# A ring of its own for the attention's squares, a product with ones for the second tokens' roots, and a new stored order in a two-layer hybrid encoder

## The chip, the cores and the metric

The kernel runs on one core of one Trainium2 chip. The metric is the device time of one execution in microseconds (us); several executions are timed and their median is given. The core has five engines that work side by side, each with its own instruction queue that is served in order: TensorE (PE: matmuls, and PEld for the load of their stationary operand), VectorE (DVE), ScalarE (ACT), GpSimd (POOL) and SyncE (SP), which in this kernel issues every DMA. Matmuls write to PSUM banks of 512 f32 per partition; everything else lives in SBUF or in device memory.

## The reference, cut to what matters

Two layers over 2,048 tokens of width 1,024. Each layer normalises x by the root of its mean square, scales and shifts it, projects it, and runs two groups of heads beside each other: four heads of gated linear attention (GLA), and four heads of differential softmax attention. Both outputs are normalised, gated, joined and projected back.

```python
h = rms_norm(x, norm_g[l]) * (1.0 + scale[:, None]) + shift[:, None]
proj = h @ w_in[l]
gq, gk, gv, glr, gz, dq, dk, dv, dz = split_columns(proj)
...
o_diff = diff_branch(dq, dk, dv, dz, qn_g[l], kn_g[l], lam, lam_init, diff_norm_g[l])
y = jnp.concatenate([o_gla, o_diff], axis=-1).astype(x.dtype) @ w_out[l]
x = x + gate[:, None] * y
```

In the differential group a head's output is the difference of two softmax maps times v, and two lines of it matter here: the output is divided by the root of its mean square, and the gate dz goes through a SiLU.

```python
attn = p[:, :, 0] - lam * p[:, :, 1]
...
o = rms_norm(o, g_out) * (1.0 - lam_init)
return o.reshape(B, S, DIFF_WIDTH) * jax.nn.silu(z.astype(f32))
```

## The kernel before, in words

**Tiles and stages.** The tokens are cut into four units u of 512, and each layer l runs over the units in turn; key = l * 4 + u counts them. For one unit the normalised input h is kept transposed, as eight tiles of 128 features by 512 tokens, each as a rounded part hhi and a remainder hlo; every weight tile w is split in the same way into hi and lo, so one product of the reference is three matmuls here. Seven projections ("items") follow: items 0 to 3 are the four softmax heads (q, k, v and gate of one head side by side, 512 columns), 4 and 5 the inputs of GLA's convolution, 6 GLA's gate. Items 7 and 8 are the output projection. The order of the items in a unit is 0, 4, 1, 2, 5, 3, 6.

**PSUM.** There are two rings of four banks: acc for the dense products, and one shared by sc (scores), tp (transposes) and po (attention outputs). Each item fills four acc banks, one per 128 tokens. The next dense product can only start in a bank that its reader has left.

**Emptying a head's banks** (head_evac). For each of the four banks t: ACT copies q and k to rw and v to Vt, ACT takes the tanh of the gate's 128 columns into a tile th, and DVE forms z = (th + 1) * gate, which reads th and the bank. That is the last use of the bank. The tile th is taken from a ring with the tag "th" of two buffers of 128 by 128.

**The end of an attention block** (pv, in attn_gen). For each 128 queries qt, once the output o_ stands in a po bank, ACT squares it with a running sum, and writes the squares, which nobody reads, to a tile junk:

```python
junk = p_t.tile([P, P], F32, tag="th", name="junk", bufs=2)
ss = p_sm.tile([P, 2], F32, tag="oss", name="oss")
A.activation(junk, o_, AF.Square, accum_out=ss[:, 0:1])
```

It is taken from the same ring as th. POOL then raises the sum to the power -1/2 (wq), and DVE scales o_ by it into z.

**Roots of the input** (root, rs_write, prep_gen, start). The sum of squares of a unit's tokens comes as 128 partitions by 4. root scales it on DVE (xms) and takes the power -1/2 on POOL into columns 0 to 3 of a constant tile rs128 (rs in the profile). The roots are wanted along the free axis and alike on all partitions, as a tile rsb of 128 by 512. Two ways lead there:
- rs_write: PE transposes rs128 into a tp bank, DVE copies four rows of it (xrr), SP writes these 2 KB to device memory (rd), and later, in prep_gen, SP reads them back broadcast over the partitions into rsb. Every unit but the first uses this way. For the units of layer 0 the squares are taken in prep_gen itself on ACT, from x; for layer 1 they come from the output projection of layer 0 (out_gen).
- in start, for the first unit: DVE multiplies an identity by the roots (dg, a tile of the ring t2 of three buffers), PE multiplies ones by dg in f32 into a tp bank, and ACT copies the bank to rsb.

Then make_h builds h: DVE multiplies x by the gain and rsb (xp), ACT rounds it with the shift added to hhi, DVE forms hlo.

**The order of the work.** The program isn't issued as it is written. Six streams (q and k preparation, attention, GLA, preparation of h, modulation, dense products) are run by a small scheduler that records each operation; Program.record keeps its reads and writes. Then Program.order plans: each engine takes the ready operation with the smallest turn, and a ring's buffers are handed out strictly in the order in which the program was recorded, so that of one tag no tile is started before those recorded ahead of it have their buffers. The turns come from the constant ORDER, a packed list of one step per recorded operation, if its length is that of the program. The result is the fixed instruction stream of each engine. In the profile nearly every instruction therefore has the same line, L362, where issue() calls the engines, and is told apart by its tiles.

```python
left_out = {t: list(q) for t, q in turn.items()}
slots = {t: [{} for _ in range(q[0].bufs or q[0].pool.bufs)] for t, q in turn.items()}
...
ahead = left_out[t].index(b, 0, 2) if b in left_out[t][:2] else N
if len(slots[t]) <= ahead or new.get(t, 0) and ahead != new[t]:
    blocked[t].append(i)
    break
```

Of the kernel before, what the change touches and what calls it, by code (L numbers as in the profile page):

```python
# [1338 lines left out]
def _layouts(x, c, w_ada, b_ada, norm_g, w_in, conv_w, w_gk, b_gk, gla_norm_g, qn_g, kn_g, lam_q1, lam_k1, lam_q2,  # L1339
# [30 lines left out]
    'gYDtAcd_peLW-sAb~<1OPH_YYOsRCU1+iqMG@NhME8jT~h%dSx#q=f&Vff-&-1vJ$o%JUz`%A6x<-6i;XUXaMEK+WB2HPPjBcg*He*HK>@DOV{bX'  # L1370
    'L)U`d>_!D7kqr{-sQQg5wx%r<@z%SHFs^SN3QCTp(od#lW$fWhs_9p*`e4DocfvT<lX_N1?6M>*0ozVNdlL;=I=Nwk?L{FL~MX*rABpWknIKSu=^'
    'ks__?b5$4HazYU$YWoV|hv(QklnpCp$RQS1*69OF~-c5|3tj+JE-|&J9Iu>yNxCa`7z`X8N;lYA(dVO*qoyuCTM>p4jf652C$`Wccn`A(3cGhD9#'
    'P-c^m|TGN%7=#PXrs=qUcm?qcIbHQ^B#mRW&%GNU^R6DuB2YL+#Me*osp`!S9@S#GS^mpAmZ=i;KqT|TgDsxj8=A1cz_<fCY%IjaXgvQg@_F|nGi'
    '0ED=oLn`kgIrqR;Om7!i>q0OI?XmOM;3_Ln@fqhb=Yn;`7E5Vm(9b5*3|_UZEZi^bpG5Z%ycbw~wxZ)i+zW9yR4AwvtRyuYzs3pC7`2}e`?+<LSh'
    'a%B<H@MrXRNau^EAJ^5u&HBBsOJMmj>ye;hLNdte7b~fQYv)8zNdKYoMXixB2OfyNiPt2jG?9=4Rqid{T55=C)D|{*Bm-yc0}VZ@rXaqe--HwL<@'
    '&P5){cRglrufBcZ<e|WlnF9y-BZrScrLDc_4PPBl3Q($xa;q5gT8j+kS@qj}qskxx23l1|B_ghw%ints^FmyQmwy02!|d*EO?hpipkY0ul|{>zv{'
    'xxXBk0;Ge+`SU?|)&b@3s7c?NM_H+9$lA!Ri82uW0y-gDUX0q2zhO}^UvN60|63Zr#BI0`rB`wa!Ck9MR5fbH4Yc&G~_<WDL*gl-@@no^i!B4;Tp'
    'yMYJRFHu&f%UIW44%r?^j?4jZa&~o-i`XlFq?7<5*NN&6Z`l-&?1G!6{~%P{lnXDNR0D^4mUdY;R1qPdF>vgjfgeh9!+~*By|QJcO3^52m<c|3DQ'
    'yY%l19b{dbw<>Vsi;$f?CWA!WO|oCplpEK~T={h6uM6cx$?tQ@c;6;2324XeeFHzamgZU4|zVMEj;#k-ayILW2Ml7_Blt+uEu42PP*28Q6I*Yx2$'
# [209 lines left out]
```

## Time and profile before

| what | value |
|---|---|
| median of 3 runs | 2417.67 us (2416.72 to 2417.84) |
| the profiled execution, whole | 2415.17 us |
| its span, first to last instruction | 2413.1 us |
| mean granted TensorE clock over the span | 0.996 |
| ACT busy | 1235.0 us (51%) |
| POOL busy | 121.1 us (5%) |
| DMA moved | 575.86 MB, mean 239 GB/s |

The profile is that of one execution. Each of its lines begins with a start time from the span's beginning and a length in us, then engine, line, operation, the tiles as out<-in by the program's names, the shape, and a count where like instructions were merged; in square brackets stands the idle time of the engine before it and what ended that. Matmuls overlap, so that the length of one is more than the distance from one to the next. Rows of the windows table begin with a stretch and its length, and tell for each engine how long it was busy in it and with how many instructions; after the engines come the granted TensorE clock as a share of full speed (PEclk), the busy share of the DMA engines, and GB/s. SPq is SyncE's queue of DMA issues.

### The profile page before, as it was taken

To read this page: it belongs to the slowest core of one execution; us is meant where nothing else is said; L and a number is where in the kernel's file an instruction comes from. 1 tells how busy PE (TensorE), PEld (TensorE's weight loads), DVE (VectorE), ACT (ScalarE), POOL (GpSimd) and SP (SyncE) were. 2 spreads that over 40 slices of the span, in tenths; PEclk is the share of its full clock that TensorE was granted. 3 is DMA by queue.
4 is the path that set the end of the run, shared out by engine and by line. 5 is a ranking of instruction groups with operands and counts; after the bars stand their busy time and mean duration, and the time that the engine had idled before them with its cause. 6 is when DMAs were issued, how large, how long until landed. Compare 5 with 4: busy or idle time off the path is not lost.

```text
span 2413.1 us, 38502 instructions
## 1 busy us (share of the span) xinstructions
PE 2369.6 (98%) x12895; PEld 1944.9 (81%) x12895; DVE 1825.1 (76%) x5156; ACT 1235.0 (51%) x2726; POOL 121.1 (5%) x400
## 2 busy tenths in 40 slices
PE   7999999999999999999999999999999999999999
PEld 5687788877888878888788887888788887888887
DVE  8878877894768967679965894668864798387894
ACT  3777643564346553445763574456533556144552
POOL 0000000000000000000000000000000000000000
PEclk9999999999999999999999999999999999999999
DMA  8578788787776879477557777676686677686773
GB/s 326 209 258 289 290 297 272 230 282 246 229 233 207 265 229 295 168 231 229 195 206 261 287 273 261 218 239 190 225 266 214 226 225 238 218 250 208 205 214 140
DMA packets 370101, 575.86 MB, mean 239 GB/s; under 512 B 191888, under 2 KB 251760, under 8 KB 366832
## 3 DMA queue, kind: packets, MB, share of 16 engines
q1 hardware_dynamic: 369904, 573.41, 72.0%
q8 instruction: 102, 1.67, 0.3%
q14 instruction: 95, 0.78, 0.1%
HBM read 418.13 MB, written 161.50 MB: 240 GB/s over the span
## 4 chain that ended last, share of the span: by engine, by line
PE 56%; DVE 4%; ACT 2%; DMA 2%; issue 1%; POOL 0%; SPq 0%; DVEq 0%; ACTq 0%; POOLq 0%
PE acc L362 37%; PE sc L362 8%; PE po L362 7%; PE tp L362 3%; DVE s L362 2%; DMA w<-wd 1%; DVE t L362 1%; ACT la L362 0%; ACT s L362 0%; ACT L362 0%; DMA out_dram<-rt 0%; DMA xp<-xd 0%; DVE ql L362 0%; DMA wr<-in_w_ada_dram 0%; DVE w L362 0%
## 5 line engine op out<-in xcount | busy, mean ns | idle before, releaser
L362 PE MATMUL acc<-w,hhi 128*128 128x512 f32 x2560 | 833.2, 402 | 9.3 <-ACT hhi L362 6.3
L362 PEld LDWEIGHTS acc<-w,hhi 128*128 128x128 f32 x2560 | 472.3, 189 | 111.7 <-ACT hhi L362 7.4
L362 PE MATMUL acc<-w,hlo 128*128 128x512 f32 x1280 | 490.1, 399 | 0.2 <-DVE hlo L362 0.2
L362 ACT ACTIVATE s<-s,mx 128x896 f32<-128x896 f32 (+15 forms) x256 | 308.4, 1205 | 344.0 <-DVE s L362 201.9
L362 DVE TENSOR_SCALAR_CACHE_REDUCE s<-sc,mx 64x64 f32<-64x64 f32 (+5 forms) x640 | 307.9, 484 | 57.1 <-PE sc L362 38.2
L362 PE MATMUL acc<-oh,w 128*128 128x512 f32 x1024 | 330.4, 396 | 1.6 <-DVE z L362 1.1
L362 PE MATMUL acc<-hhi,w 128*128 128x512 f32 x960 | 319.0, 399 | 1.2 <-DVE z L362 1.1
L362 PEld LDWEIGHTS acc<-w,hlo 128*128 128x128 f32 x1280 | 239.9, 189 | 47.0 <-issue 1.3
L362 PEld LDWEIGHTS acc<-oh,w 128*128 128x128 f32 x1024 | 190.6, 188 | 43.3 <-DVE z L362 1.8
L362 PEld LDWEIGHTS po<-Vj,s 128*128 128x128 f32 x1536 | 204.2, 196 | 10.8 <-DMA s<-ad 1.0
L362 PE MATMUL po<-Vj,s 128*128 128x128 f32 x1536 | 211.5, 280 | 0.9 <-DMA s<-ad 0.6
L362 DVE TENSOR_SCALAR_CACHE_REDUCE s<-sc 128x512 f32<-128x512 f32 (+4 forms) x256 | 157.8, 621 | 69.0 <-PE sc L362 44.2
L362 PEld LDWEIGHTS acc<-hhi,w 128*128 128x128 f32 x960 | 178.3, 188 | 36.9 <-DVE z L362 1.9
L362 DVE SCALAR_TENSOR_TENSOR s<-s,r 128x512 f32<-128x512 f32 (+3 forms) x320 | 202.6, 666 | 2.7
L362 PE MATMUL acc<-ol,w 128*128 128x512 f32 x512 | 198.5, 395 | 0.0
L362 PE MATMUL acc<-hlo,w 128*128 128x512 f32 x480 | 188.8, 397 | 0.0
L362 PE MATMUL sc<-Kj,qh 128*128 128x512 f32 x384 | 156.7, 413 | 0.8 <-ACT vN L362 0.3
L362 PE MATMUL sc<-Kj,ql 128*128 128x512 f32 x384 | 150.7, 397 | 0.0
L362 DVE SCALAR_TENSOR_TENSOR t<-ub,vec,t 128x512 f32<-128x512 f32 x192 | 140.6, 746 | 6.8 <-ACT t L362 5.7
L362 POOL MEMSET s<- 64x64 f32 x256 | 37.0, 145 | 2079.2 <-PE po L362 1266.0
L362 ACT CAST w<-raw 128x512 fp32r<-128x512 f32 x160 | 97.5, 621 | 83.3 <-PE acc L362 67.0
L362 DVE TENSOR_TENSOR w<-raw,w 128x512 fp32r<-128x512 f32 x160 | 108.5, 687 | 39.0 <-ACT w L362 37.8
(185 smaller groups left out, 3603.8 us busy)
## 6 DMA issues: line engine op xcount, KB each, us to landing
w<-wd SPq DMA_DIRECT2D x416, 512.0 KB, 4.3
wd<-w SPq DMA_DIRECT2D x144, 512.0 KB, 4.0
raw<-in_w_all_dram SPq DMA_DIRECT2D x80, 512.0 KB, 5.0
...
wr<-in_w_ada_dram SPq DMA_DIRECT2D x128, 128.0 KB, 3.6
...
```

The source lines that it names most:

```text
L362: getattr(self.engines[e], method)(*[real(a) for a in args], **{k: real(v) for k, v in kw.items()})
```

## The change

Three things change. The squares junk get a tag and a ring of their own, with one buffer; the ring of th keeps its two. The way by a product with ones becomes a function rs_spread, which start calls and which prep_gen now also uses for key 1, the second 512 tokens of layer 0: for that unit the transpose, the copy, the write and the broadcast read fall away, and root and rs_spread stand where the read was. The other six units keep rs_write. ORDER is replaced as a whole: 19,399 steps in place of 19,400.

```diff
+    def rs_spread():
+        dg = t2()
+        pb = tp()
+        V.tensor_tensor(dg.rearrange("p (t n) -> p t n", t=TT), ident.unsqueeze(1).to_broadcast([P, TT, P]),
+                        rs128[:, 0:TT].unsqueeze(2).to_broadcast([P, TT, P]), op=ALU.mult)
+        T.matmul(pb, ones, dg, start=True, stop=True)
+        rsb = rs_tile()
+        A.copy(rsb, pb)
+        return rsb
+
...
             yield pe(0, 8.0)
-            rs_write(key, ss)
-        rsb = rs_tile()
-        SY.dma_start(rsb, RD[key].broadcast_to([P, UT]))
+            if u > 1:
+                rs_write(key, ss)
+        if key == 1:
+            root(ss)
+            rsb = rs_spread()
+        else:
+            rsb = rs_tile()
+            SY.dma_start(rsb, RD[key].broadcast_to([P, UT]))
...
         root(ss)
-        dg = t2()
-        pb = tp()
-        V.tensor_tensor(dg.rearrange("p (t n) -> p t n", t=TT), ident.unsqueeze(1).to_broadcast([P, TT, P]),
-                        rs128[:, 0:TT].unsqueeze(2).to_broadcast([P, TT, P]), op=ALU.mult)
-        T.matmul(pb, ones, dg, start=True, stop=True)
-        rsb = rs_tile()
-        A.copy(rsb, pb)
+        rsb = rs_spread()
...
-            junk = p_t.tile([P, P], F32, tag="th", name="junk", bufs=2)
+            junk = p_t.tile([P, P], F32, tag="junk", name="junk", bufs=1)
...
 ORDER = (
...
```

More of the change, by code (lines that the diff above doesn't have):

```diff
@@ L1370 @@
[L1370 to L1379, printed above, removed]
@@ new lines @@
+    '9Eb?IHQcDI9#uJ&DHn<2}}6t3Mu=X#`rG-^GZZ<|8evYZwMIu2gt@#9Bh@dY}aPNS+Q!R|WPi9>VInEuL6uM{=NqZAvLL$Er1w>KpLm}r4+y+r1!'
+    'u}+o&KWg>p1tc_HK(3Z}A^?<O_<IWZ-46O|NjHKue@P5p($|bpOLqqV1Da8$S^~CqXbu|#g$(ak;csV%VfJmi(H1Y}cPMinc&5c6$X`a&{Fw&5y$'
+    'paMq;bpub(NS^ZFhS8r$Y4NM>yoq0czf#Kz{ldPT-()O2b{;jJ<Qj!d73)yCP+aj;UR=47)TXSz~*y!fzeLS(;8BJ{r(8#FfwRo-hNJ_$}_X!s7J'
+    'cVHzZ~gex^%LyAQF@kU^HoVL@l)A=R#%B@xr>e?!2jBl|kvl5l2&byFB5|=H#J7^GiT%8G-GGzc1b>||i^(h|pe<SBtc8rUuk%)re$ai|>^FQ3~N'
+    '*i}*sUFWWx}B)rUhCq%LnEu|o^|%*sDl%uWhd!3>7wR}ik5-XJ|O{_6L+-RA!@1cTDs({DX(r=F<nb^b`mzrA#g65d9hpT)b4C1*2L)~LnF-WV91'
@@ new lines @@
+    'u_(?@xp?6Wu-4%5&bL_MM#5H2+a5%y=Au4kVi9*~9=#x{VbDFqp-j)C`<UAFnB;BY&Yenb$jf#nsm+pdgS;~~reB>p58L!zJWg>G3@h~T8+Jp^CD'
+    '??Wn52l%PIv#P@-;Ps#Pg}WSr?2m3YAvW4oeJ6MqDN8wgn4m#KvB9+Ge-SIpZ>TfcKHqT0{GDz&<IuV~n_XSsbV;(CFdg4Op`POwIogj&S{$5{x4'
+    '^qw%9Sw$5UsIZmqr%{2^Dn$=wwV9TGdj|hi*D-AS39LAyM+2EmT~}@_>R0954G3#ODW=vya2JkSY9nyn6nR-Q1oU_K3crFb3DXU2~UI>3XfGU_5G'
+    'CkK+Qrvhd_zei4AVyLEctdqhQ0f__3)Re9<6nB-52VN3sVw`o}-`l|7dSxsxwnS}IM+6$1(Y9IO|#i(TC6r4g#)HXsUA137)e+e0(Nlkyz45mL6A'
+    'yd8|X2`gVxBiYFGJjWEv7#M~%MsBTDVFq>;xqgns<eXE#3LJmKEi64mTP8a3YYEaO=2xNtJJh#ns`aMOW_OIAr4z+at^f>uYPY-dJwOG4LZ+4!K|'
@@ new lines @@
+    'YsI3tVR_j5sV$W+(#Ot8kSRS*^MymP(8%vx1SGX@{zQNs~)ae==%*eeg$omEs{ARo2senQNvHh20VK*z7r7Kj+}%N)dPuj^%ANjZN2l4+;n{;kJ%'
+    'C8bd6exwi9Y|(X%aUK;0b{YjVEt&a@{vnb>+wf1*p`hTey}hy|^=UBAA7I~Y^#e<vl_m8??%{1X_j47uV!B3)L`0d4wIs-oiy?~cQLRbv?&$GWQM'
+    '97@j^@<`9;$xZ0IpUn3>zmicL)xPf;;GB;FOE8D4}Hh;-+CxcVDWzRRgyI)^WV#soR<n58A!-*_@wbVx|o=XMWJy7aoMWdT25{(P3%Y%_P6S=QM3'
+    'VvY}<2eTeo+jucnmE3m44L7VdeWBiL$@CY-;vCu?Umz^z$ruGnmKt$bdAMhia%*|{57u1~mE^+6v5?lK?8l2W!U1vDY3h(YgM$+XCP}a*hIWcJQy'
+    'W|Tj`AY1ZYt$%4y6an6(vHMVXVc$bAm|G9$nGCQ%sW!Ssl>cr1h6m|tQ?pf7+uAorJ@Ogp~W~Yb&Zlfiv>=&90tS3CNct{?m5p8ju+qFiy2c~!CQ'
@@ new lines @@
+    '0BW)w!6X3x&wFVYPUr_UO;X%$$g7w@sgJ~AVw{*UMY0nk9fh)uh589%OZ6{Z~Rk6)ObIz&LGxR&OIf>jJtf3&Q~OeqoLgGj|={|HJ<u_q0A=1467'
+    '|IQpp2Pc+7J^e4viabX(<P=H9u_EkO8jQ#=WG}?!;7?gn@@@}xf$INg0hGGIiYJOxq;z@K$Rs$NA<TXLgLf=kx&@(MFY&gDAq{p^qDbzEd+Ip2Xi'
+    '&|r+%E>)_ae!te)Py{k#rplV`TbsK>ik#KJDiJr`7L1fc~MctHO=Bz7wv3#bVg1_doyx=bdLzEachxMMwiVT9o($ms1|*m>td_V2gUiz{5p>f!hy'
+    '*Y=k|b>@p0ln8+Vp;h_`#pd<?a2<P}DMJx8vwP8&w);x#<r}diSN67s*-7xhJ`(;tqx>r(q+GdUrIlYHg-wL}r0*l6e4s$a7x#2^!c(|UV?cDCdb'
+    '%>RB$8<0Y*|H}EYB~d4hW4#sNXdIFl&A^g6Z!Oa6Scqg)FVc&j$|6ts6GVGwK>cnDRQ-wWnkKLrvN1RN7gYQmklZnzj@mY16hI|MTc)r-T+{LSs9'
@@ new lines @@
+    'j%W`(Xp$%*O2zswMMrStfOCJ*UXD%$lKikB;fph<X=z?#Tt6^qxC2MX{jMI8Hk=En>2jR5)g(lL^yKVi9}!~R>CPcN5qZnWgd6+<?_L4Hc)WOg!?'
+    'Ec+Auzg^rudiOiQaRg4LXp>#7DBo?DD<@%NctYD99|m&Ic?w-CC9UpKc>saNLfUJOt1$tvM)mH7E}A-hikGV+cNR$j<s?_*1H67Nq7IR1|5F2u#k'
+    'y1fB4PVUtOCkc4|UFpO6L=>_H0*@w1h_C7z^T?{hr)Fj-F9A!3d9un2k`l8N*?<0O?;8eUYtSagx;PH3opEA+rsqn;F5^b4rg7R)wd_`O;uSC1Q`'
+    'p=Cr1L_Z?Rpn^Yb)3w~|Ud#UtQ-Q%A~SD-CH!MzW9o(ER3o)rlUKM@aq`W{Sy)jE@2=BOY1v|Ug>>gv&g*Rv0v+g%ft#}$w{9h2N3J7b%AkpOs8O'
+    'OXLoJBr}rgX?PKWOC82_WnYcMDFmNy1*r37~I?(L~gyk0d)-ES1{Hp_(?XvA1^cVe38O8feq<<jC=U#@Y(RDBesgCN5t?-iQy!+WvmC1@KaAM4Tc'
@@ new lines @@
+    'A{arv_sNRu|wQ34(3yv+xYo-}`QQQurHG4}Z83-|pHpS=#=#()MjVf7AAHC5vHHmN~NL*`|x3FSun1kMhznMa--ec-u!gs+1Cm#?}x$$+`c-Gh+b'
+    'Avd0qU(Wx7EyEG^uP2de>5o`2b_rHmSIZH5JOlwD-~1~mp~eObm^j4+00?V3j(G*`u;6^cZ&NEq7|^p{I5+F=c8~gsx1rtXoBm(lu6(W_W&Rcm4Q'
+    '0sp)<{pWNa7QKQkme!sGKTd4O=Q4G%2x(|6ff)DI;k)vO(TYe)yfQ>b7K<<1zJ1dT>`E7Sbc!c~~YuRxt>!ww&L@d8vXif@&i_QIJ*5lZ3_kp?>$'
+    'rTdE16z;5NbRpkV1#4VZ!3a|y~$fi6-^*EO-@p}pmBB6OM-<<pkh7-s}g5ImhGpx%e%Tjby8FNb21&op(0dkxkxSPMdE2cxK^VO+|z`|rB$;1_6e'
+    '8tpKT=+l~B6`e^om_AJgqAp!6<pX#m&s;g9Y<tMb&vz)cW57CRiwobC>hU<0)#cIpC&Kd3+l0K=9G5F=Jf^?!CL=0pi{IhlnGb@()qr57l%J^fgr'
@@ new lines @@
+    '!V>|vdyHF77>Q2SYLo}NPb^*JSSKnr)^TUquGMWQF<_X4WX+{G=UbIcbdF^k$HD9Jzx7Ma5<o&oivp7=N;(0QM&9I7s|DO_Iti5B8sn-R}_#;BZg'
+    'muB3K?}!cR(FLLHrh}U?yotS#;4Z@}=LLo;`9|x<WX1*CHrIy}t`ne>Q&uqNIfh<Qs^sqZl{+7sc#r9!mjq>H!r=gCTgX#8okU_pqpc<FEh=x;YW'
+    'y0ce{sPc+$WP9OtSGKeO-8UpP*G?)Pq~Ih`zr*%ZiTjFbRj@z<lgcg~lB=_@jA5q(4S)(l~xMA3fWSvXV9#M}{+~Cu$)!h1MrjA{0S9A)o`io$j4'
+    'xIlpxP2E?jTe}P8#Kf9>AJ6BHkj)TqRU3LZ1$5flu)q0dP`zl}zt`hq1Uw{zoHYs}v#f@kJrI-EhP#oLoq(<4QqGl|8VH@(K$RtT;QBcqDG&YMv`'
+    'VYpS{Bn<Yo|LLGWSx{fbF5Ir`ORRsL)Zolcw5`AW^_|4@PR0JT1lMy&0p*=IDwU9`Cg|X9E38w+yxe>p-Fb7=fhWT#fYzx?dFY%-P3i~m*vTbLIC'
@@ new lines @@
+    '$QIYD=K-?$ndFQuB>yHpnVSvLK#y6#Ec`Q=N$*Dr++!Hn9W)PK<QAw>9Z#`G{P)8s{6+JD;+ywBlWfjEo_Pb?6{<am|?pyql*C@zUBhYa-k#?UgR'
+    'z^U|roTN5XOZfGg12i;|fK|7nFy)<s9DtuRX<M-SdDX!;7s5MvdjE$C-B!_|!X6b1O}szWLWy6*RPa}0{3?YZCTii9?+3IUoHjz|&KzbNHJ5yg^s'
+    'r@Eia)1HgHt5*Z=7V=Y6<J9la9+Z5yZV<&DMAUB`CHhJxt9Dt2BJcTx~#3p)jNv)PRgN#RV7E2y$4?OfxQv>YK{A#f0M|#p<m)Z&9>xo0q^}0z}T'
+    'LPIpP6Kaz4N?`p6sr=@&NlC_LLGJbGvFi4*k&i&pO?B|e1!Zn{4T^_crjJbOK_+efunrN8aJ<-%ae@`z-#P~<qQM8&|!m^0+^!9OwIbRkOI~uuZY'
+    '!fXug>l|Ixj596oa!vTi2`?uq$TrtR9#y$;vtEr;=;TtSne_aesOpru2tp#X65Rm|0GxpfJ9sMP7)H<oP4QW>3B;riYOzQhhE7M@rc#~KopnqJU%'
@@ new lines @@
+    'bssoS~7uPOcB!x+-AtnrqPlKl<06kNgqB@P0vy#>Z1zZ;J%|AuHNcd9x-YQSTgw(0VE!JnUzMa-{R0f84h^h2*$Fn;MXhEtn#QI+65CPo%g^vEou'
+    ')GOAjUC^37l$4Z+J{~ioCT9z(M-))^wX8J<&^bdSq0{K@Md>Q?KZF_HiwX%k>ClH3*bd)z>%Bg!e;vq3T4=?ZOm2_6H=^67q{C_|++yz5IOmPmuE'
+    'K6+wRdKC_9(hbj~KA0|6{qB&|lpunS6Zd&AQM1=xM5e1yp%?*)SCKkGf%ukx<`3HJPv_a)FB>Le}V()@&C+#*^BsI(13#OSp@ywQEwZ@2Vw`N7c_'
+    'R)=_Hcd$Y`-_RvDRDIcPXG$kW?^9GSBA<n@mksT}Qo0`B1y0av(@hpqnJRjZA-3Kq%Y?@Tv&7Av}n|PbIi_b%tzM_;Hd@WjjB!DE}Bv0^Mv(K_48'
+    '-EV;A&8$qLAwM0Rb|FXz*cHTQGox52GS>BM~$~4;;Axi_CR}+ty)#iN12)=HFriJWdpIRJcpmgdJ_rYx@qL+x$cZ(RE<bjCsb=tTK|;{Jg|m@;4Z'
@@ new lines @@
+    'mUty$re>Qgoj&QvIIlE=D3htWzf_EY4BlW{Y{Wv6wt3y(sAe;&a6IE)iA#$&)5_P3M+59%nEfH;Mt1r0bU?u+CE-)=abk_kxN!aGMm1A+G&aHtlY'
+    'Zja3Li`5^@DKZC<aYe>e7tW0IztUC$&kr#$Wn19usD!_>5X1K$_PoNB+aLCHNW5?asGLsF#XOjq+eQ4YSii8}gvN5HP4-fwh%3b0B`Iped;y|lbb'
+    '^c|<>S_3AI&iOdE0T^Dv=&kF78YSjh?zw_Tj{p)kS?;IaY0~fc&+p-5-n7j*T@HMbO@(bj}dB6G;QcteB^1a7Y+t3AUL&9{(b73GlIDfX27_7f3p'
+    'V=5`nS@@A%d0Ao8)ivTHOP!o?(vlATIDNyoWc&M#qR9+PfWT@z=l@7AiEo=QjO<W<x8u0qsVbJw9L{7ZiS!be<nKt9bCWs=7q8*(jM;jcgpLo9bV'
+    'K{`DqdQ7;5Z&hAWgEFwWi4>=iYY%SZlBGPmLZ-r`O4<E0PFKylorl)jmpBc57xfa3ClH2C#{+R7r_%vPg?sCQAKY4=Z|`q?q0yg@oT;|BxOLY*}>'
@@ new lines @@
+    'IZoiTXDrp8J`TnaR;|A)}3%T9J!(~<#qvd3Wm8&~9nk=jNTcwaucPcjdOOyTs|TgF#GRB<i2s?$SZ^zdv?3W5i(kyFVPvOjD6JCppe`g?@bZ_KQq'
+    ')F!C*C2vD{<YU#Cefp=SDA_kO`Ynl7<(VcgTMJK2HeO+r?$u+W*KY56YP>=vHzTp6NdB_hBKH@iM@lnsc<0op=t*)<cs+a?DYbo|_GknbGx}0=ga'
+    'U12W_FUCXZ+1P`=wr<jy)|F22cEbWJOcRQWJMaeTaGQhdQ3eFx@doU}9wM`Vki4D8H$)Gd9sh#<&)<d}FqhG|`2GG2w&vQ*%|Ws<s?Ltam#TG(C`'
+    '$Gg&z8u6y%l1r}0)=Ak!W|0mK5S7g%`V51W}{-r202-5|T6@cqBNgv?ZVohEvr-=7j(_?%tL^reP@!0}>JDSG~3aAuu=p=bwjm!sgp7L&h;(6Fkl'
+    'rnYg;l(7M@MCX-m>9MO#R|mwdC*8M3Voo~cG0DyUgu`!7KxT9<IoxMK5g^K0rOu8k?v^A$}XNxeQfWbjy1k@v*$%hO4Hr=1tl(aCj;Zl%B)MVRMJ'
@@ new lines @@
+    'Q!!(C(UL?~2Jnx?=wJc?b<Ff)_CM1wC;!;Oqrv912l_9-Fq0l%-WpZLhOKEBR3Ie~uu9hv<NRS}A@Jx<-Yl-ekX(FYj(gM~v?XnxKdtqxXnbzz=>'
+    'vO8^W-sg^AVE`auv)90U{c&6#_7<wic75V_)WUD#*ntq!6)5O;rWZY@4)FaIasYE^*Jzy7P2R)i`#$v4Zz-R*)4ByFTWJ3{0B+ml?cPrTS43xZUk'
+    'fy)JZ(PM0D{PaxV)2CEgEa}wr^CKe`YB0p)HIhN+Q;EkIoi+njYwpavIAi8(@>vd1=e+utpDq5YMV_o>cb?eevM}MH7t)==)ssdG+s!2LLYG&*vv'
+    'b<M-bQ$gyUg#^{fPk{|c*I=!U<Ja2X~rAf>Kd?^*T5_g-;wYvdD1oRU%k<NT%WSTJx$|$04=Jx_bzr-XAtS-sK^q!Bl2I>wW4A+nwlXf19<TTGFE'
+    '#`EhIxD41jr6Lls@a*sRvS9|Rgo=&TLVYhFbH^z(ZtR>T<6x4uZo|@19>%Vz+$$yz@j9mrrMscFaMeg;t$%Ed&UrwkYA5%=|D+&P=^BIRMC=ck?L'
@@ new lines @@
+    '7T`#5ps6S*I)3T+xwk;t4LE+0X8duC-n2|o)9Xa;99o?^F%zGKlP;0!qPJAr$)r)35}0_FQD0C;>XW(H=>8+08Fc5D!cz@(NpIv~6`4*G-7<pXL}'
+    '(0S+ZC^o@4hp5v<O9*zo>w)`l{U*emOvHZQQ1&;e$?;5Z#pvL{+M<gt@Dq~_*?mmr_>>k?TO2;vSw_54EMuCsy3MDqMNU5xyjCXsF7+sAu9k$=nr'
+    '={gKTu<-rLWWy`!Th7j_x(7cU~Z;(oUsvZd>qhqS)1dO$&n)JA=U-CIf~2-A&s&QLsNRRp?b|?=3wU#=ndtU^u*X!!J9;ke+8wU6fR)LH{IqHKfO'
+    'hzDd5#6GPQ2G1qq6cQ7wtD&d<f!L8FX9Po?Qw+kMl5k%dk5C-jd;r10kZJfshiK&T?0$j8|s*Pncn;IBUvQ=>@?x1YY&5aKt4|MFhFB>ynZ~Pb%{'
+    'e?xFFiak#n581ha+7U$ntpnel&{{+NcLu%BtM&2@N&g&xt$Z0d97ZV4{3ZwG^sB8IaQifXN2#1?nLV9t97G>%%$paUlsRbmn2co$bHk}mE_s*l6z'
@@ new lines @@
+    'k$W$zoG=tCMXQeSwQGaM1zxEI$42rICGvBgT2hWs{ZjPKzC1UqRqkXJ1po3^rNlXprGYpPL3oWb387Ms9ARZFZyg50yd7LAp9Kq#Lc&t{5mr^uIM'
+    'IEfaWGx(u+dKtAn^xNn<@P8<rpvMtPYnA$K*ZqMka51f7D{$P>IXS`xi00`sQ+LZLgcNi4w&J`~JTA{=x7oy1!OMgZYq3y$BvRKL=LD@<*4<gDuf'
+    '(AX6-hO4DB|y?4qo>sPrZq5m-6N?v3Y3iBv7lGJU<?!EITjd#Dw6U98KMtHJ%&v0;mN4>LGNObbmTYKd-G4OnTLCKdrOuoSE4G<c}drM>nHkA>H='
+    'X{`RN|lJ66xN6@4`GNnmanP{N|;w}zf9#WaGBusVz1aB%v&E=Me3-#U)FTQA-ET;aTbTiLaQ@CaQ{77`*TRBvs0Y(0Wd~FdvoiWUKW;Pix%Yr1gP'
+    '8+N^LlIdY=1pdtSu*)=G%^Q9nU|b(HnjQo*i<@XGDPd%s~lI~=_#84_x-x|&z^aMYTeT-*7k_tnKy`5u}^VELf5(M1OjKnue9--O3`3+<+;wFVeR'
@@ L1567 @@
+    '}M)Wm1X@V12t8;d3I6ALDSpplE~>qWvIO<mr?+dY@e4^HBWVt-B4BwWLDVc_G%bBf0yNN||yDWVkP-thnccfH#o>^RMX00E?r0gkT%gD~jkvBYQl'
+    '0ssI200dcD'
 )
```

326 lines of the change are left out of this document (134 added, 192 removed).

## The prediction

> **What bounds the kernel now.** I read the page first, then the windows table, coarse and fine, then the order of time around the two places that the table picked out.
>
> ```profile
> span 2413.1 us, 38502 instructions
> PE 2369.6 (98%) x12895; PEld 1944.9 (81%) x12895; DVE 1825.1 (76%) x5156; ACT 1235.0 (51%) x2726; POOL 121.1 (5%) x400
> ```
>
> PE is busy 98% of the span, so whatever costs or saves PE time is the time. But a mean hides stages, and a busy PE need not run at the full clock. Five stretches (their length, then PE, PEld, DVE, ACT and POOL busy, each with its count, then the granted clock, the DMA share and GB/s):
>
> ```profile
> 40.00:95.00 55.00, 54.73 (x252) 42.90 (x250) 52.32 (x130) 37.05 (x74) 0.62 (x4) 1.00 0.66 240
> 95.00:116.00 21.00, 16.75 (x75) 12.03 (x68) 17.76 (x76) 14.13 (x49) 2.63 (x10) 0.76 0.53 190
> 116.00:234.00 118.00, 117.44 (x694) 96.02 (x693) 95.59 (x304) 84.81 (x225) 9.98 (x33) 1.00 0.73 259
> 234.00:242.00 8.00, 4.45 (x15) 3.44 (x14) 7.24 (x16) 5.20 (x13) 1.19 (x3) 0.79 0.96 337
> 242.00:2413.00 2171.00, 2150.89 (x11795) 1773.87 (x11793) 1623.31 (x4556) 1077.70 (x2342) 104.42 (x340) 1.00 0.72 235
> ```
>
> Between 40 us and the end PE is full and at full clock except in two short stretches, 95 to 116 and 234 to 242, where it is partly idle and the granted clock falls to 0.76 and 0.79. All of the rest (242 to 2413) holds 2171.00 - 2150.89 = 20.1 us of idle time, in crumbs. The first 40 us are the start, which the change leaves alone. The two stretches, cut finer:
>
> ```profile
> 98.50:104.90 6.40, 3.89 (x19) 2.11 (x16) 6.01 (x28) 5.25 (x19) 0.83 (x3) 1.00 0.43 170
> 104.90:111.60 6.70, 5.03 (x18) 3.75 (x18) 5.64 (x26) 4.22 (x17) 1.18 (x6) 0.50 0.75 275
> 111.60:115.20 3.60, 3.54 (x11) 2.87 (x12) 3.50 (x15) 1.17 (x4) 0.62 (x2) 0.50 0.00 0
> 115.20:125.00 9.80, 9.80 (x54) 8.14 (x53) 4.43 (x8) 7.31 (x14) 0.69 (x2) 1.00 0.03 10
> 234.40:238.00 3.60, 0.06 (x1) 0.00 (x0) 2.89 (x6) 1.97 (x7) 0.92 (x3) 1.00 0.98 317
> 238.00:241.50 3.50, 3.49 (x8) 2.80 (x9) 3.45 (x9) 2.65 (x6) 0.00 (x0) 0.51 0.97 366
> ```
>
> First stretch: idle 2.51 + 1.67 + 0.06 = 4.2 us. The clock stands at 0.50 in the two later rows, so half of their busy time, (5.03 + 3.54) / 2 = 4.3 us, is lost as well: 8.5 us. Second stretch: 3.54 us idle, then 3.49 us at 0.51, of which half, 1.7 us: 5.3 us. Without the slow clock the two would be worth 4.2 and 3.5. The Trainium skill ("TensorE: Matmul & The Clock Gate", the part on what is actually happening) says that PE falls to half rate after about 3.4 us of too little activity and needs a busy window to come back. The rows agree.
>
> **What holds PE in the first stretch.** The dense matmuls of the third head (w by hhi into acc) need an acc bank that the second head's evacuation has left. ACT, PE and DVE in order of time:
>
> ```profile
> 97.86 0.28 ACT L362 COPY Vt<-acc 128x128 f32<-128x128 f32 x1
> ...
> 102.00 0.28 ACT L362 ACTIVATE junk<-po 128x128 f32<-128x128 f32 x1
> ...
> 107.89 0.28 ACT L362 ACTIVATE junk<-po 128x128 f32<-128x128 f32 x1
> ...
> 110.75 0.28 ACT L362 ACTIVATE junk<-po 128x128 f32<-128x128 f32 x1 [0.84 <-PE po L362]
> ...
> 111.01 0.27 ACT L362 ACTIVATE th<-acc 128x128 f32<-128x128 f32 x1
> ```
> ```profile
> 97.12 0.40 PE L362 MATMUL acc<-w,hlo 128*128 128x512 f32 x1
> ...
> 111.66 0.79 PE L362 MATMUL acc<-w,hhi 128*128 128x512 f32 x1 [0.52 <-DVE z L362]
> ```
> ```profile
> 111.31 0.29 DVE L362 SCALAR_TENSOR_TENSOR z<-th,acc 128x128 f32<-128x128 f32 x1 [0.60 <-ACT th L362]
> ```
>
> The last copy out of the banks ends at 98.14. What is left is the tanh of each bank (th) and the product that reads th and the bank (z). The tanh starts at 111.01, directly behind the third square of the first head's attention output (junk, 110.75). Both tags share one ring of two, and a ring is handed out in the order in which the program was recorded, so the tanh can't pass the squares, and these wait for the attention (the third for po, 0.84 us). For 111.66 - 97.12 = 14.5 us no dense matmul runs.
>
> **What holds it in the second.** The first matmul of the second 512 tokens, back along its chain:
>
> ```profile
> 187.52 1.03 POOL L362 TENSOR_TENSOR rs<-xms,mhalf 128x4 f32<-128x4 f32 x1 [1.42 <-DVE xms L362]
> ```
> ```profile
> 221.87 0.27 PE L362 MATMUL tp<-ident,rs 128*128 128x128 f32 x1
> ```
> ```profile
> 222.79 0.28 SPq L362 DMA_DIRECT2D rd<-xrr  x1
> ...
> 230.75 0.41 SPq L362 DMA_DIRECT2D rsb<-rd  x1
> ```
> ```profile
> 235.06 0.68 DVE L362 TENSOR_TENSOR w<-raw,w 128x512 fp32r<-128x512 f32 x1
> 236.45 2.08 DVE L362 SCALAR_TENSOR_TENSOR xp<-xp,A,rsb 128x512 f32<-128x512 f32 x3 [0.71 <-DMA rsb<-rd]
> ```
> ```profile
> 237.24 1.39 ACT L362 ACTIVATE hhi<-xp,B 128x512 fp32r<-128x512 f32 x2 [1.60 <-DVE xp L362]
> 238.01 0.78 PE L362 MATMUL acc<-w,hhi 128*128 128x512 f32 x1 [3.55 <-ACT hhi L362]
> ```
>
> The roots are there at 188.55. They are transposed at 221.87, written to memory at 222.79, and read back spread over the partitions from 230.75, behind other work of SP's queue. DVE's first product with rsb waits for that read until 236.45; hhi and then PE follow.
>
> **The change part by part.**
>
> *Own ring for the squares.* It adds and removes no instruction. The four tanh may follow the copies, from about 98.1; with 0.28 us for each tanh (the x1 row of junk has the same shape and engine, 0.28) and 0.29 for each z, the first bank is free near 99 and the rest within 1.5 us, some 12 us earlier than now. Dense matmuls can then fill the idle time, and the clock need not fall. At the upper end all 8.5 us come back. Against that: DVE is busy 6.01 of 6.40 us there, and the weights' low halves (0.68 us each) and z must pass through it; what the attention waits for, DVE, stays. At the lower end half comes back, 4.2 us. I take 7.5, nearer the upper end: a weight tile feeds 12 matmuls, which at full clock (six records in 1.52 us below, 0.4 of it the length of one: 0.22 us from one to the next) is 2.7 us of PE, so DVE owes the dense stream only a quarter of PE's time. The new ring has one buffer: a square waits for the square before it, which is on the same in-order engine: 0.
>
> ```profile
> 245.20 1.52 PE L362 MATMUL acc<-w,hhi 128*128 128x512 f32 x6
> ```
>
> *Spread by a product.* It removes a transpose (0.27 us shown, among others that overlap it), a copy of four rows on DVE, one small write and one broadcast read on SP. It adds DVE, PE and ACT work, as at the start of the kernel, where the same lines stand:
>
> ```profile
> 14.89 0.69 DVE L362 TENSOR_TENSOR t<-ident,rs 128x512 f32<-128x512 f32 x1
> ```
> ```profile
> 15.68 1.34 PE L362 MATMUL tp<-t,ones 128*128 128x512 f32 x2
> ```
> ```profile
> 17.05 0.59 ACT L362 COPY rsb<-tp 128x512 f32<-128x512 f32 x1 [0.90 <-PE tp L362]
> ```
> ```profile
> 233.63 0.83 PE L362 MATMUL po<-Vt,s 128*128 128x128 f32 x6
> ```
>
> PE pays between 0.9 and 1.3 us: 1.34 is shown near an idle PE; the six po records, f32 like the product, take (0.83 - 0.27 of the last one's tail) / 5 = 0.11 us each, and four times the columns in two records make 0.9. Less some 0.1 for the transpose, I take 0.8, the PE being full then. DVE's 0.69 and ACT's 0.59 come between 188.55 and 234, where DVE is busy 95.59 of 118.00 us and ACT 84.81: 0, and 1.3 us if that cover were gone. The chain from the roots is then about 2.6 us long, with 45 us of room. It uses a t2 buffer (three in all) for some 2 us instead of none, and SP's queue loses two entries: 0.
>
> The Trainium skill ("Perfetto Trace Analysis", Transposes) speaks against this edit: it wants a transpose rather than a standard matmul. By that rule the edit costs the 0.8 us and brings nothing; by the rows it buys the wait.
>
> What comes back: with rsb early, DVE can make the first xp as soon as an hhi buffer is free. Next in line is the w product that ends at 235.74. If the first matmul needs that one, PE starts at about 236 in place of 238, and 1.5 us are left idle but not the slow clock: 2.0 + 1.7 = 3.7 back. If not, all 5.3. I take 4.8, since w has four buffers and the first tile of an item is hardly the last one made, and hold 3.7 as the lower end.
>
> *New order.* Every place of 19,399 recorded operations may shift (19,400 before). Its only prey outside the two stalls are the 20.1 us of crumbs after 242, and there the clock is 1.00 already. No row tells its sign. I take 0, and a fifth of the crumbs, 4 us, on both sides.
>
> **The sum.** 7.5 + 4.8 - 0.8 = 11.5 us. The profiled execution takes 2415.17 us as a whole, so 2403.7 against it. The median of the three runs, 2417.67, lies 2.5 us higher; on that scale it is 2406.2, and I say 2406.
>
> **The rivals.**
> 1. *DVE takes over* between 98 and 112. For it: DVE's 6.01 of 6.40 us. The tanh go early, but z and the low halves stand behind the attention's reductions, the clock still falls, and only 2 us of the 8.5 return. With 4.8 - 0.8, 6 us in all, 2412; with the lower end 3.7 it is 4.9 us, 2413, at the edge of what shows. Against: in the next 9.80 us (115.20 to 125.00 above), where the dense stream runs, PE is full with DVE busy only 4.43 us.
> 2. *It doesn't do what it says*: the new order puts the tanh behind the squares as before, or the product just ahead of its use at 234. Then one stall is left: gain 4.0 or 6.7 us, 2411 to 2414.
> 3. *Slower*: a new stop of PE. The new order lets PE's in-order queue stand for a DMA or an evacuation for 3.5 us, and the clock drops for 3.5 more. One such stop costs the 5.3 us of the second stretch. After 242 there is none now (clock 1.00). Two stops take back 10.6 of the 11.5 us; the third makes it slower, by 15.9 - 11.5 = 4.4 us, 2422, and with a fourth, 2427, it shows. Against it: no such stop has arisen in 2171 us of the order now.
>
> **How the numbers follow.** About 0.2%, 4.8 us, is what a measurement of this kernel can tell from no change: faster is under 2412.8, slower over 2422.5. Chances: the forecast (one or both stalls mostly gone) 0.66; the first rival 0.14, half of it each side of 2412.8; the second 0.13, again split about evenly; the slower rival 0.07. Faster: 0.66 + 0.07 + 0.05 = 0.78; slower 0.07; the rest, 0.15, within. Range: the low end is both stalls gone whole and the order's 4 us, 13.8 - 0.8 + 4 = 17 us, 2401, and a little for the scale between profile and runs: 2400. The high end takes the first two rivals in, 3 us of gain with an order that costs a little: 2415.
>
> **What would show it.** In the changed profile: a tanh that starts within some 2 us of the last Vt copy near 98, and dense matmuls into acc between 98 and 111; clock 1.00 in the windows near 105 to 115 and after the change of tokens; no rd write or rsb read for the second 512 tokens, a second pair of f32 products with ones at 0.9 to 1.3 us, and the hhi wait of 3.55 us gone or under 2; idle time after 242 us still near 20 us. I am wrong if the clock still falls in either place, if DVE is what the bank waits for (z late, th early), or if the crumbs after 242 grow by over 5 us.

## The result, and the profile after

The changed kernel takes 2403.26 us in the median of four runs (2401.78 to 2404.02); the kernel before took 2417.19 beside it (2415.85 to 2417.84). The ratio is 0.9939 with an interval of 0.9926 to 0.9951. The forecast was 2406, in a range of 2400 to 2415. A second set of runs of the same changed kernel gave 2405.49 against 2418.33, ratio 0.9943 (0.9930 to 0.9955). Ratios are turned into us below by multiplying them with 2417: the two sets are then 14.7 and 13.8 us gained, where the forecast's sum was 11.5.

The head of the changed kernel's page:

```profile
span 2399.8 us, 38461 instructions
PE 2362.6 (98%) x12896; PEld 1943.4 (81%) x12896; DVE 1824.5 (76%) x5156; ACT 1231.4 (51%) x2727; POOL 128.6 (5%) x400
```

The share of PE is again 98%: the page alone doesn't show where the time went. The table of windows, cut at the same times as before (length, then the engines' busy time and counts, then the granted clock, the DMA share and GB/s), does:

```profile
95.00:116.00 21.00, 20.58 (x113) 15.97 (x112) 18.10 (x76) 16.98 (x56) 2.11 (x7) 1.00 0.70 252
116.00:234.00 118.00, 116.03 (x685) 93.62 (x683) 102.61 (x319) 87.93 (x232) 12.59 (x37) 1.00 0.74 261
234.00:242.00 8.00, 7.47 (x33) 5.69 (x33) 7.90 (x22) 5.63 (x13) 0.70 (x2) 1.00 0.79 321
242.00:2399.00 2157.00, 2139.23 (x11751) 1768.59 (x11749) 1615.97 (x4539) 1070.90 (x2336) 110.37 (x340) 1.00 0.73 236
```

In the first stretch PE is busy 20.58 us in place of 16.75, and the clock stands at 1.00 in place of 0.76; in the third it is 7.47 in place of 4.45, and 1.00 in place of 0.79. Both stalls are gone. The idle time after 242 us is 17.8 us (20.1 before), so the crumbs have hardly moved.

The first stall in the changed kernel, told by the summary of the tile th from 90 to 113 us (engine, operation, count; shortest, median and longest in ns; start of the first and of the last):

```profile
L362 ACT ACTIVATE th<-acc x4: 268/336/338, 95.3 to 100.6; 128x128 f32<-128x128 f32 x4
L362 DVE SCALAR_TENSOR_TENSOR z<-th,acc x4: 277/282/289, 95.6 to 102.1; 128x128 f32<-128x128 f32 x4
```

The last of the four tanh starts at 100.6 where the first of the four started at 111.01 before, and the four z follow by 102.1. The squares come when they come, for instance at 108.20, and hold nobody. Dense matmuls run where none ran for 14.5 us before:

```profile
104.18 0.86 PE L362 MATMUL acc<-w,hhi 128*128 128x512 f32 x3
...
109.96 0.63 PE L362 MATMUL acc<-w,hhi 128*128 128x512 f32 x2
```

The second stall, on DVE, then PE, then ACT in order of time:

```profile
211.60 0.68 DVE L362 TENSOR_TENSOR t<-ident,rs 128x512 f32<-128x512 f32 x1
...
216.38 0.75 DVE L362 SCALAR_TENSOR_TENSOR xp<-xp,A,rsb 128x512 f32<-128x512 f32 x1
```
```profile
213.86 1.02 PE L362 MATMUL tp<-t,ones 128*128 128x512 f32 x2
...
234.64 0.73 PE L362 MATMUL acc<-w,hhi 128*128 128x512 f32 x2 [0.42 <-DVE t L362]
```
```profile
108.20 0.27 ACT L362 ACTIVATE junk<-po 128x128 f32<-128x128 f32 x1
...
214.92 0.59 ACT L362 COPY rsb<-tp 128x512 f32<-128x512 f32 x1
...
217.16 1.47 ACT L362 ACTIVATE hhi<-xp,B 128x512 fp32r<-128x512 f32 x2
```

rsb is there at 215.51, and the first hhi start at 217.16, where before the first xp with rsb waited until 236.45 and PE until 238.01. The wait of 3.55 us for hhi is gone; PE's longest wait between 205 and 245 us is now the 0.42 shown. Writes to rd and reads into rsb are six each in place of seven, the first write at 356.6 us, so none is left for the second 512 tokens. So every sign that the prediction asked for is there. What the profile after can't say is which of the three edits brought how much.

### The profile page after: what moved, and what is told of

It reads as the page before. It is cut to its first block, busy times and chain, and to the rows that moved or that the text cites. A ratio compares the mean times of both kernels' runs of the same rounds, so it can differ in the third digit from the quotient of the medians.

```text
span 2399.8 us, 38461 instructions
## 1 busy us (share of the span) xinstructions
PE 2362.6 (98%) x12896; PEld 1943.4 (81%) x12896; DVE 1824.5 (76%) x5156; ACT 1231.4 (51%) x2727; POOL 128.6 (5%) x400
## 4 chain that ended last, share of the span: by engine, by line
PE 53%; DVE 8%; DMA 2%; ACT 2%; issue 1%; POOL 0%; SPq 0%; DVEq 0%; ACTq 0%
PE acc L362 35%; PE sc L362 8%; PE po L362 7%; DVE s L362 4%; PE tp L362 3%; DMA w<-wd 1%; DVE t L362 1%; ACT s L362 1%; DVE xp L362 0%; DVE w L362 0%; DVE hlo L362 0%; ACT qh L362 0%; DVE vN L362 0%; DMA rsb<-rd 0%; DMA wd<-w 0%
## 5 line engine op out<-in xcount | busy, mean ns | idle before, releaser
L362 ACT CAST w<-raw 128x512 fp32r<-128x512 f32 x160 | 97.8, 622 | 86.3 <-PE acc L362 57.5
```

The costliest lines, as they stand in the source:

```text
L362: getattr(self.engines[e], method)(*[real(a) for a in args], **{k: real(v) for k, v in kw.items()})
```

## The experiments

**The two edits under the old order.** The first three kernels keep the stored ORDER of the kernel before. With the ring alone that order fits as it is; where the spread is in, the program has one recorded operation less, and the place of the missing one is taken out of the turns.

The ring alone:

```diff
-            junk = p_t.tile([P, P], F32, tag="th", name="junk", bufs=2)
+            junk = p_t.tile([P, P], F32, tag="junk", name="junk", bufs=1)
```

> The kernel before with the squares' own ring alone: the roots of the second tokens go through memory as before, the order is the old one, step for step. Theory A (each edit lifts its own stall, whatever the order): the first stall's 8.5 us come back for the larger part, 7.5 us less than before (4.2 to 8.5), the tanh starts near 98, and the clock stays at 1.00 near 105 to 115; the second stall stays. Theory B (the edits only make room, and the new order brings the gain): under 3 us less than before, and dense matmuls still pause for over 10 us after 97.

Measured: 2411.30 us against 2417.19, ratio 0.9975 (0.9967 to 0.9984), 6.0 us gained. Its windows, first the first stall, then the second:

```profile
90.00:100.00 10.00, 9.93 (x56) 7.46 (x55) 8.90 (x27) 9.88 (x30) 0.00 (x0) 1.00 1.00 346
100.00:110.00 10.00, 7.19 (x39) 4.89 (x38) 9.55 (x40) 7.47 (x28) 2.02 (x7) 1.00 0.61 219
230.00:234.00 4.00, 0.36 (x4) 0.17 (x2) 3.21 (x7) 2.29 (x7) 1.08 (x3) 0.87 1.02 309
234.00:240.00 6.00, 6.00 (x15) 4.70 (x16) 5.92 (x14) 3.40 (x7) 0.00 (x0) 0.52 0.97 380
```

The second stall stays, and its slow clock even lasts longer in this profile: PE runs at 0.52 for all six us from 234, where it ran at 0.51 for 3.50 us before. In the first place the clock holds at 1.00, but PE is still idle 2.81 us of the ten from 100 to 110. Why, ACT, DVE and PE tell:

```profile
102.45 0.43 ACT L362 ACTIVATE th<-acc 128x128 f32<-128x128 f32 x2
```
```profile
95.75 0.29 DVE L362 SCALAR_TENSOR_TENSOR z<-th,acc 128x128 f32<-128x128 f32 x1
...
109.59 0.29 DVE L362 SCALAR_TENSOR_TENSOR z<-th,acc 128x128 f32<-128x128 f32 x1
```
```profile
103.36 0.40 PE L362 MATMUL acc<-w,hhi 128*128 128x512 f32 x1
...
109.93 0.73 PE L362 MATMUL acc<-w,hhi 128*128 128x512 f32 x2
```

One bank is freed early, by the z at 95.75. The next two tanh are done by 102.88, but the z that frees the next bank starts at 109.59, 6.7 us later, and the dense matmuls stop between 103.36 and 109.93. DVE isn't waiting: it is busy 9.55 of 10.00 us with the attention's work, which has smaller turns in the old ORDER. The tanh pass the squares now, but all z except the first stand in DVE's queue nearly where they stood when the tanh were late.

The spread alone (the new start and prep_gen, the squares still in the tanh's ring):

```diff
+        turn = np.arange(len(step), dtype=float) + np.cumsum(step.astype(int))
+        turn = np.delete(turn, 1849)
```

> The kernel before with the spread by a product alone; the squares stay in the tanh's ring. Old order: the three operations of the spread take the places of the transpose, the copy and the write, and the place of the read is dropped. Theory A: the second stall goes, 4.8 us less 0.8 for the product: 4.0 us less than before (2.9 to 4.5), first matmul of the second tokens with no wait of 3.5 us and the clock at 1.00 after it. Rival: xp or w comes next and PE waits for that nearly as long; under 2 us less than before, and the clock still falls behind 234.

Measured: 2415.38 against 2417.19, ratio 0.9994 (0.9985 to 1.0003): 1.5 us, not to be told from nothing.

Both edits under the old order (ring and spread, as above):

> Both edits of the change, with the old order (the one place too many dropped as in the run of the spread alone). Theory A: the two gains add up, 11.5 us less than before, and at most 3 us are left to the new order. Theory B: under 6 us less than before, and the new order brings the other 8.

Measured: 2410.69, ratio 0.9972 (0.9961 to 0.9983), 6.8 us. So about half of what the whole change gains is missing when the old order stays. The second stall of this kernel, on ACT and on PE:

```profile
219.93 0.72 ACT L361 ACTIVATE hhi<-xp,B 128x512 fp32r<-128x512 f32 x1 [0.20 <-DVE xp L361]
222.62 0.72 ACT L361 ACTIVATE hhi<-xp,B 128x512 fp32r<-128x512 f32 x1
...
232.57 0.72 ACT L361 ACTIVATE hhi<-xp,B 128x512 fp32r<-128x512 f32 x1 [0.80 <-DVE xp L361]
```
```profile
230.21 1.62 PE L361 MATMUL acc<-w,hhi 128*128 128x512 f32 x6
...
233.25 0.50 PE L361 MATMUL acc<-w,hlo 128*128 128x512 f32 x1 [1.43 <-DVE hlo L361]
```

The first two hhi come early, at 219.93 and 222.62, and PE begins with them at 230.21. But the next hhi comes at 232.57, and PE stands for 1.43 us for hlo. That is the first hlo of these tokens, and DVE starts it at 232.45, only 1.9 us earlier than the 234.30 in the kernel with the ring alone, whereas the first hhi is 13 us earlier. (In the whole change the first hlo starts at 218.48.) The old order makes the first two hhi early and leaves the rest of h, the first hlo included, nearly where it was. Part of what the spread brings is handed back a few us later.

**Another control for the ring: a third buffer, still shared.**

```diff
-            th = p_t.tile([P, P], F32, tag="th", name="th", bufs=2)
+            th = p_t.tile([P, P], F32, tag="th", name="th", bufs=3)
...
-            junk = p_t.tile([P, P], F32, tag="th", name="junk", bufs=2)
+            junk = p_t.tile([P, P], F32, tag="th", name="junk", bufs=3)
```

> The kernel before with the shared ring of tanh and squares enlarged from two buffers to three, which takes the same 512 bytes per partition as a ring of its own; old order. If the order in which a ring is handed out holds the tanh back (theory A), a third buffer lets at most one tanh past: within 2 us of before, the last tanh still behind the third square. Rival: two buffers were too few, and a third one brings most of what the own ring brings, 4 to 7.5 us.

Measured: 2418.60, ratio 1.0003 (0.9994 to 1.0012). The same number of buffers in all as in the change, and nothing gained. ACT shows why:

```profile
102.29 0.28 ACT L362 ACTIVATE junk<-po 128x128 f32<-128x128 f32 x1
...
108.17 0.28 ACT L362 ACTIVATE junk<-po 128x128 f32<-128x128 f32 x1
...
110.10 0.26 ACT L362 ACTIVATE th<-acc 128x128 f32<-128x128 f32 x1
```

The first of the four tanh, at 110.10, still comes behind the squares at 102.29 and 108.17, and the other three come behind the third square. Under the old order, then, it is the order in which one ring is handed out that holds them, and a third buffer doesn't help.

**The order without, and with one of, the edits.** The new ORDER has one entry fewer; where the spread is left out, one turn is put in.

```diff
+turn = np.insert(turn, 1849, turn[1848])
```

The new order alone:

> The kernel before with the new order alone: shared ring, roots through memory; the places of the spread's three operations go to the transpose, the copy and the write, and the read gets the last of them once more. If the new order were a gain of its own: 0 to 8 us less than before. Theory A gives it 0, 4 either way. Theory C: the order was found with the tanh free of the squares, so that with the shared ring the tanh of many heads now stand behind late squares: slower than before, by 5 us or more, with stops of PE at which the clock falls.

Measured: 2473.54 against 2417.06, ratio 1.0238 (1.0223 to 1.0254): 57.5 us slower. PE's waits in it:

```profile
PE po L361 <- ACT s L361: 9.5, 12, 1.9
PE tp L361 <- DVE s L361: 9.3, 13, 3.0
...
PE acc L361 <- ACT hhi L361: 8.1, 3, 2.8
PE acc L361 <- DVE z L361: 8.0, 9, 3.2
```

(us in total, times, longest.) The head of its page tells what the time is made of:

```profile
PE 2392.0 (97%) x12895; PEld 1961.5 (79%) x12895; DVE 1826.8 (74%) x5156; ACT 1232.0 (50%) x2726; POOL 124.6 (5%) x400
```

Its span is 2472.5 us. PE is idle for 80.5 us of it, 37.0 more than before, and busy for 22.4 us more with the same 12,895 matmuls, while the mean granted clock is 0.988 in place of 0.996. At the first stall and at the head after it, ACT's queue shows the old picture, a tanh directly behind a square, and PE waits for z, at the second place 3.17 us:

```profile
114.21 0.28 ACT L361 ACTIVATE junk<-po 128x128 f32<-128x128 f32 x1 [0.16 <-PE po L361]
114.48 0.27 ACT L361 ACTIVATE th<-acc 128x128 f32<-128x128 f32 x1
...
147.18 0.28 ACT L361 ACTIVATE junk<-po 128x128 f32<-128x128 f32 x1
147.45 0.27 ACT L361 ACTIVATE th<-acc 128x128 f32<-128x128 f32 x1
```
```profile
150.78 0.80 PE L361 MATMUL acc<-hhi,w 128*128 128x512 f32 x1 [3.17 <-DVE z L361]
```

The new order and the ring, with the roots still through memory:

> The changed kernel without the spread: own ring and new order, the roots of the second tokens through memory. Theory A: the second stall is back, 4.0 us over the changed kernel, 2407, and the clock falls once. Rival: the new order asks for the read early enough, and no stall comes back; then it is 0.8 us under the changed kernel, 2402 to 2403, and the spread has brought nothing that the order would not.

Measured: 2408.60, ratio 0.9967 (0.9957 to 0.9978), 8.0 us gained. The only difference to the kernel 57.5 us slower than before is the ring of junk: its own, with one buffer, in place of the shared one with two. (A shared ring of three was not run under the new order.) Its first stall, and what is left of its second:

```profile
95.00:116.00 21.00, 20.57 (x110) 15.86 (x109) 18.14 (x73) 17.59 (x56) 2.11 (x7) 1.00 0.71 252
...
230.00:236.00 6.00, 5.50 (x19) 4.34 (x20) 6.00 (x12) 3.32 (x8) 1.01 (x2) 0.72 1.04 413
```
```profile
222.19 0.37 SPq L361 DMA_DIRECT2D rsb<-rd  x1
```
```profile
229.88 0.73 PE L361 MATMUL acc<-w,hhi 128*128 128x512 f32 x2 [2.91 <-ACT hhi L361]
```

The first row equals that of the whole change (20.57 and 20.58 us busy, clock 1.00): for the first stall the ring and the new order are enough, and the spread has no part in it. The second stall remains: the read is issued at 222.19 instead of 230.75 before, but PE still waits 2.91 us for hhi, and the clock falls to 0.72.

The new order and the spread, the squares back in the tanh's ring:

```diff
-            junk = p_t.tile([P, P], F32, tag="junk", name="junk", bufs=1)
+            junk = p_t.tile([P, P], F32, tag="th", name="junk", bufs=2)
```

> The changed kernel with the squares back in the tanh's ring: spread and new order. Theory A: the first stall is back, 7.5 us over the changed kernel, 2411. Theory C: as with the order alone, the new order leans on the free tanh in more than one place: over the kernel before, 2417, by 5 us or more.

Measured: 2471.02, ratio 1.0226 (1.0212 to 1.0240), 54.6 us slower. All eight combinations, in us against the kernel before (minus is faster):

| | neither edit | ring | spread | both |
|---|---|---|---|---|
| old order | 0 | -6.0 | -1.5 | -6.8 |
| new order | +57.5 | -8.0 | +54.6 | -14.7 and -13.8 |

The intervals are some 2 to 4 us to each side. Read by columns: with both edits the new order is worth 7.0 to 7.9 us; with the ring alone 2.0, within the intervals; without the ring it costs more than 50. Read by rows: under the old order the spread adds 0.8 us to the ring, under the new one 5.8 to 6.7.

**What the product costs.** The changed kernel with the product made nine times into the same bank; the result is the same.

```diff
+        turn = np.insert(turn, 1848, [turn[1847]] * 8)
...
+        for _ in range(1 + more):
+            T.matmul(pb, ones, dg, start=True, stop=True)
...
+            rsb = rs_spread(8)
```

> The changed kernel with the product with ones for the second tokens made nine times in place of once, into the same bank, all with its place in the order; the result is the same. PE is full there, so eight more products cost eight times the price of one: 0.9 us each is 7.2 us over the changed kernel, 2410.5; 1.3 us each is 10.7, 2414. If PE had room there, under 2 us.

Measured: 2408.77, ratio 0.9969 (0.9958 to 0.9981). Against the two sets of the change this is 6.3 to 7.2 us for eight more, 0.8 to 0.9 us each. The summary of the products' records (as for th above):

```profile
L361 PE MATMUL tp<-t,ones x18: 592/593/593, 214.6 to 221.9; 128*128 128x512 f32 x18
```

18 records start within 7.3 us, 0.43 us apart, so 0.86 us for a product of two records, whatever the record's own length of 0.59. The price in the time and the spacing in the trace agree, and PE is full there. By the time alone, with intervals of some 3 us to each side, 1.3 us each could hardly be excluded; the spacing decides.

**Where the order's gain lies.** Both edits in each of two kernels; the first takes the new turns for the first 3,700 recorded operations, which reach to about 440 us, and the old ones behind, the second the other way round.

```diff
+was = np.delete(np.arange(len(old), dtype=float) + np.cumsum(old.astype(int)), 1849)
+turn[3700:] = was[3700:]
```

> Both edits, with the new order for the first 3,700 recorded operations (to about 440 us) and the old one behind. If the new order's 8 us (the changed kernel against both edits in the old order) come from the two early stretches, where the spread now stands early enough: 11 to 14 us under the kernel before, no clock drop between 100 and 300 us, but the weak place near 1,190 us still there. If they come from the rest: 7 us under before, as in the old order.

```diff
+turn[:3700] = was[:3700]
```

> Both edits, with the old order for the first 3,700 recorded operations and the new one behind: the counterpart. If the place near 1,190 us, where the old order lets PE idle by 2 us and more and the clock falls in some profiles, is the larger part: 10 to 12 us under the kernel before. If the early stretches are it: 7 to 8 us under before.

Measured against 2418.33: 2402.72 with the new order first, ratio 0.9933 (0.9920 to 0.9945), and 2413.26 with the old order first, 0.9973 (0.9962 to 0.9984). The whole change, run beside them:

> The changed kernel unchanged, timed beside the two mixed orders on the same chip: 0.994 of before.

It took 2405.49, 0.9943 (0.9930 to 0.9955). So the whole of the order's gain sits in the first 440 us, and the new turns for the other four fifths of the span bring nothing that shows. The window of the first stall, first with the new order first, then with the old:

```profile
95.00:116.00 21.00, 20.57 (x109) 15.90 (x108) 18.11 (x72) 17.70 (x56) 2.12 (x7) 1.00 0.71 255
```
```profile
95.00:116.00 21.00, 18.32 (x92) 13.69 (x92) 18.13 (x78) 14.03 (x52) 2.60 (x10) 0.84 0.54 198
```

With the old order first, PE loses 2.3 us more here by idling than with the new order first, and (1 - 0.84) * 18.32 = 2.9 by the clock. With the tile th summarised as above, the old order's z are late:

```profile
L363 DVE SCALAR_TENSOR_TENSOR z<-th,acc x4: 280/284/289, 95.5 to 110.5; 128x128 f32<-128x128 f32 x4
```

The last z starts at 110.5, against 102.1 in the whole change.

**The slow clock by itself.** The kernel before with fifteen f32 products of ones and the identity, which change no result, put into PE's wait of the second stall, in a bank that the next item overwrites.

```diff
+                        if (l, u, item, j) == (0, 1, 0, 0):
+                            for _ in range(15):
+                                T.matmul(banks[0][:, 0:P], ones, ident, start=True, stop=True)
...
+turn = np.insert(turn, 2094, [2001.0] * 15)
```

> The kernel before with 15 small f32 products of ones and identity (128 columns, some 0.22 us each) put into PE's queue ahead of the second tokens' first dense product, in the bank that this one then clears; they change no result. They fill the wait for hhi and shorten nothing. If the slow clock behind 238 us comes from the idle 3.5 us: the clock stays at 1.00 there, the first eight dense products take 0.23 us each in place of 0.43, and the time falls by up to 1.7 us, about what the interval is wide. If it has another cause: the clock falls all the same and the time stays or grows.

Measured: 2417.68 against 2418.33, ratio 0.9998 (0.9989 to 1.0007). The wait is filled, and the clock behind it doesn't fall. On PE, and in the window that stood at 0.51 before:

```profile
235.60 3.51 PE L361 MATMUL acc<-ident,ones 128*128 128x128 f32 x30
239.49 1.19 PE L361 MATMUL acc<-w,hhi 128*128 128x512 f32 x4 [0.37 <-ACT hhi L361]
```
```profile
238.00:241.50 3.50, 3.09 (x18) 2.27 (x17) 3.49 (x8) 2.05 (x3) 0.00 (x0) 1.00 1.02 369
```

So the slow clock does come from the wait before it, as far as one profile of each kernel tells. Its cost, 1.7 us by the prediction, is not shown by the time, for the interval reaches 2 us to each side. The two traces do show a cost: from the start of the first dense matmul behind the wait to that of the tenth it is 241.77 - 238.01 = 3.76 us before and 241.99 - 239.49 = 2.50 us here, 1.3 us less. That this profile has its first dense matmul at 239.49 and not at 238.01 is mostly not the work of the filling: the last matmuls ahead of the wait, po, already start at 234.94 here, and at 233.63 before.

## Why the prediction came out as it did

**What bounds the kernel: right.** PE's time is the time, and it was lost in two places. Both are full at full clock after the change, and the time fell by about the sum of what they held (8.5 + 5.3 = 13.8 us, or 12.9 less the price of the product, against 13.8 and 14.7 measured).

**The ring: mechanism right, size off.** The claim that the tanh stood behind the squares because of the order in which one ring is handed out is shown by two runs under the old order: a ring of its own gains 6.0 us, a third shared buffer nothing. But of the 7.5 us that I took, 6.0 came with the ring itself. The prediction let z follow each tanh at once. Under the old order the second and third follow 6.7 us after they could, because DVE has other work with smaller turns. That is the first rival's picture, th early and z late, though milder than priced (it let 2 of 8.5 us return): the clock held in that profile (with the old order put first it fell to 0.84 in the same stretch), and DVE was full by the order of its work and not by its amount, since in the changed kernel z is on time with DVE as busy in that stretch (18.10 us of 21.00; 17.76 in the kernel before).

**The spread: mechanism right, size off.** The product's price, 0.9 us (0.8 less the transpose), was right to the tenth by the spacing. The 4.8 us of return were not seen without the new order: 1.5 net with the spread by itself, 0.8 on top of the ring, each some 2 to 3 us uncertain. The step "hhi and then PE follow" looked at hhi only. Under the old order the first hlo still comes late, as do the third and later tiles of h, and PE stops again 3 us after its start. With the new order the spread is worth 5.8 to 6.7 net, more than the 4.0 that I took.

**The new order: the step that failed.** "I take 0", because "its only prey outside the two stalls are the 20.1 us of crumbs". The crumbs were indeed no prey: 17.8 us are left, and the new turns behind 440 us bring nothing that shows. But the sentence asked only what an order could gain outside the stalls. Inside them it was needed to collect what the edits made possible: it brings z forward in the first and the rest of h, the first hlo above all, in the second. That is 7.0 to 7.9 us, more than either edit brings under the old order, and my own 4 us to each side don't hold it. The sum came out near because it gave the edits the whole stalls, and so counted the order's part under their names: 7.5 + 4.0 forecast, 6.8 + 7.0 to 7.9 measured. That the total fits is luck in this respect: the edits as priced bring little more than half of it.

**The rivals.** The second rival held half a truth: under the old order the edits do half of what they say. The third, a new order that makes PE stop, happened in full where the ring is missing: 57.5 us, eleven times what I priced for one stop, spread over waits that are 1.9 to 3.2 us at the longest in the rows shown. With the ring it didn't happen. At two heads the trace shows a tanh behind a square again; what holds PE in the other places is not followed through here, and shown is that the ring of junk alone decides between +57.5 and -8.0.

**Left open.** How the order's 7 to 8 us divide between the two stalls is read from profiles of single executions, and not from runs that change the order in one stall alone. The old order with the spread is one order of many, too: its three new operations took the turns of the transpose, the copy and the write, and other turns might have brought more. And the cost of a slow clock of 3.5 us shows in two traces, not in the time.
